# Hybrid decoder layer, one core: when and into which buffers seven weight tiles are split, and the order of the third token tile's normalisation

## The chip, the cores and the metric

One core of one Trainium2 chip. The metric is the device time of one execution in microseconds (us), as the median over runs. A core has a TensorE (PE, matrix multiplications), a VectorE (DVE), a ScalarE (ACT), a GpSimd (POOL) and a SyncE (SP); the last two also issue transfers. Each engine works through its own instruction list in order, so an instruction that waits holds up all that stand behind it on that engine.

## The reference, cut to what matters

One decoder layer on 512 tokens of width 1024, all in float32:

```python
h = layer_norm(x, g_in, b_in)
z = h @ w_in          # split into GLA q, k, v, r, a gate, MLA latents, merge gates g0, g1
y_gla = (gla(...)) @ w_o_gla     # gated linear attention, 4 heads
y_mla = (mla(...)) @ w_o_mla     # latent attention, 8 heads
m = sigmoid(g0) * y_gla + sigmoid(g1) * y_mla
x1 = layer_norm(alpha * x + m @ w_out)
out = layer_norm(alpha * x1 + relu(x1 @ w_ff1) ** 2 @ w_ff2)
```

The parts that matter here are the first `layer_norm` with the latents' product behind it, the two gate products g0 and g1, and the output product of GLA, called yg.

## The kernel before, in words

**Split weights.** TensorE takes every operand as a high and a low part. A weight tile of 128x1024 is loaded (`wraw`, or `wq` when it is kept for later sums), ACT copies it rounded into the high tile (`act(..., AF.Copy)`), DVE subtracts to get the low one (`vtt(..., op=ALU.subtract)`), and three products are made: high with high, high with low, low with high. In the trace every ACT and DVE instruction that goes through a helper carries the helper's line, L111, so they are told apart by tile name. In the products the lines are L313, L314, L315 (tokens by rows, `gemm_tm`), L279, L280, L281 (`gemm_fm`) and L1299, L1300, L1301 (`unit`).

**The stream.** All weight tiles stand in one list, `stream`, in the order of use. `pump(i)`, called when tile i is wanted, loads up to two tiles ahead on SP and splits one tile ahead, or two where the entry says `"ahead": 2`. The pair of tiles that a split writes has a home:

```python
HOME = {"w": ("whi", "wlo"), "r": ("wraw", "wraw"), "a": ("xh", "xl")}
TAG_W = {'wraw': 3, 'whi': 2, 'wlo': 2}
```

Home "w" is a ring of two high and two low buffers: a split must wait until TensorE has read the tile before the last. Home "r" takes two of the three buffers of the raw loads. Home "a" is the large pool, 24 buffers of 128x1024 shared with activations, kept weights and others; a buffer taken from it makes a later user of the same slot wait.

**Seven products for eight.** g0, g1 and yg are made by `unit`: each weight is cut into four blocks and seven products (11, 21, t1, 22, t2, t3, t4) replace eight. The t tiles are sums of blocks. Each product has two tiles, g = 0 and 1, of 24 matmuls each. A sum is made either by DVE (`u_sum`, `wq<-wq,wraw`) or by a transfer on POOL's queue that adds while it writes: `u_load` (L1272 loads, L1274 accumulates) for the t1 and t3 of g1 and yg, and `u_acc` (L394 to L398) which turns g1's t2 into its t4 as soon as t2 has been split.

**Order of the stages around the change.** Token tiles 0 and 1 are normalised and transposed; then the latents' product runs with tokens 0 to 255 (`gemm_tm` with i = 0 and 1) while the generator `ln_in1` normalises tiles 2 and 3 (`ln_rows`: statistics, variance, a power on POOL at L483, the bias `nmr`, then two halves) and transposes them (`ln_transpose`, L505). `ln_in1` also orders two splits behind the variances (`stream[tt + 3]["gates"]`). Stage two, about 250 to 297 us, is g1's products; stage three, to 340 us, is yg's, mixed with the MLA query products (qr, qn, kn, mv). ACT and DVE serve all of them: splits, the gates' activations (`gt`, `u`, `e`) and the operand sums (`hx`, `so`, `ogT`, `hraw`).

Of the kernel before, what the change touches and what calls it, by code (L numbers as in the profile page):

```python
# [19 lines left out]
P = 128  # L20
T = 512
D = 1024
NT = T // P
# [29 lines left out]
def tile_hybrid_block(ctx: ExitStack, tc: tile.TileContext, I, out, dbg=None):  # L53
    nc = tc.nc
# [49 lines left out]
    chain = {}  # L104
# [18 lines left out]
    mm = nc.tensor.matmul  # L123
# [17 lines left out]
    xt = []  # L141
# [12 lines left out]
    ident = ca[:, 0:P]  # L154
    identJ = rev(ident)
# [13 lines left out]
    stream = []  # L169
    st = {"dma": 0, "spl": 0, "gates": ()}  # L170
# [120 lines left out]
        tick(width)  # L291
        return accs

    def gemm_tm(pls, xs, n, evac, width=None, tts=range(NT), guard=None, ks=None, accs=None, new=None, fine=False):
        accs = {} if accs is None else accs
        ticks = [0]
        share = n <= 256 and len(pls) == 1 and len(tts) == NT
        nk = pls[0]["nk"]
        for k in ks or range(nk):
            ws = [weights(pl, k) for pl in pls]  # L300
            first, last = k == 0, k == nk - 1
            for tt in tts:
                c = slice(tt * P, (tt + 1) * P)
                xh, xl = xs[k][:, 0, c], xs[k][:, 1, c]
                for j, (hi, lo) in enumerate(ws):
                    if first:
                        if share and tt % 2:
                            accs[tt, j] = accs[tt - 1, j][:, 256:]
                        else:
                            accs[tt, j] = (new or MM)()  # L310
                    o = accs[tt, j][:, :n]
                    opens = first and not (share and tt % 2)
                    mm(o, xh, hi[:, :n], start=opens, stop=False, skip_group_check=share)  # L313
                    mm(o, xh, lo[:, :n], start=False, stop=False, skip_group_check=share)  # L314
                    mm(o, xl, hi[:, :n], start=False, stop=last, skip_group_check=share)  # L315
                ticks[0] += 1
                if fine is True or fine and ticks[0] % fine == 0:
                    tick(width)
            if not last and not fine:
                tick(width)  # L320
        if evac is None:
            return accs
        if guard:
            guard()
        todo = [(tt, j) for tt in tts for j in range(len(pls))]
        for i, (tt, j) in enumerate(todo):
            evac(tt, j, accs[tt, j])
            if i == len(todo) // 2 - 1:
                pump(pls[-1]["idx"][-1] + 1)
        tick(width)  # L330

    HOMES = "wwrawarawawawa"
    half = LAT // 2
    PL = {}
# [61 lines left out]
    def plan_unit(*seq):  # L396
        for key, op in seq:
            for g in range(UNITS[key][2]):  # L398
                PL[key, op, g] = len(stream)
                e = {"nk": 4, "n": 256, "res": False}  # L400
                if op[0] != "t" and (op, key) not in HELD:
                    e["dmas"] = [(slice(0, 4), u_src(key, int(op[0]) - 1, int(op[1]) - 1, g), None)]
                else:
                    e["src"] = lambda q=(key, (op, g)): WQ[q]
                    if key == "g0" and op in ("t1", "t2"):
                        e["ahead"], e["home"] = 2, "wr"[g]
                if op == ("t1" if key == "g0" else "22"):
                    e["post"] = lambda raw, q=(key, "t1", "t2", g): u_sum(*q, WQ[q[0], ("22", q[3])] if q[0] == "g0" else raw)
                    if key == "f1":
                        e["post2"] = lambda raw, q=(key, "12", "t3", g): u_sum(*q, raw)  # L410
                elif op == "21" and key == "yg":
                    e["post"] = lambda raw, g=g: u_sum("yg", "t2", "t4", g, raw)
                elif op == "t2" and key == "g1":
                    e["post"] = lambda raw, g=g: u_acc("g1", "t2", "t4", g, "21")
                elif op == "t2" and key != "yg":
                    e["post2" if key == "f1" else "post"] = lambda raw, q=(key, "t2", "t4", g): u_sum(*q, WQ[q[0], ("21", q[3])])
                stream.append(e)
# [53 lines left out]
        fb += nb  # L471


    def ln_rows(src, dst, mv, on_act=False, behind=None):
        bst = S([P, 2, 6], F32, "bst")
        for j in range(2):
            with ExitStack() as gates:
                if behind is not None:
                    gates.enter_context(tc.issue_after((behind if j else st["var"]).ins))
                bns(bst[:, j, :], src[:, j * T:(j + 1) * T])  # L480
        bna(mv, bst)
        st["var"] = vts(mv[:, 1:2], mv[:, 1:2], LN_EPS, None, op0=ALU.add)
        st["pow"] = gtt(mv[:, 1:2], mv[:, 1:2], mhalf[:, 0:1], op=ALU.pow)  # L483
        if on_act is not False:
            nmr = S([P, 1], F32, "nmr")
            chain.pop("dve", None)
            behind = st["nmr"] = stt(nmr, mv[:, 0:1], -1.0, mv[:, 1:2], op0=ALU.mult, op1=ALU.mult)
            for j in range(2):
                c = slice(j * T, (j + 1) * T)
                if j in on_act:  # L490
                    st["norm"] = act(dst[:, c], src[:, c], AF.Identity, scale=mv[:, 1:2], bias=nmr)
                else:
                    st["norm1"] = vts(dst[:, c], src[:, c], mv[:, 0:1], mv[:, 1:2], op0=ALU.subtract, op1=ALU.mult)
        else:
            vts(dst, src, mv[:, 0:1], mv[:, 1:2], op0=ALU.subtract, op1=ALU.mult)
        return behind

    def ln_transpose(rows, g, b, outs, hf, alt=False, n="h0"):
        tk = slice(hf * 256, (hf + 1) * 256)
        for k in range(NK):  # L500
            if len(outs) <= k:
                outs.append(A([P, 2, T], F32R, n) if n == "h0" else (B([P, T], F32R, n), B([P, T], F32R, n)))
            p = MM() if alt and k in (4, 5) else PX()
            for i in range(2):
                nc.tensor.transpose(p[:, i * P:(i + 1) * P], rows[2 * hf + i][:, k * P:(k + 1) * P],  # L505
                                    identJ if hf and n == "h0" else ident)
            tmp = B([P, 256], F32, "lnt")
            hi, lo = part(outs[k], 0, tk), part(outs[k], 1, tk)
            ha = act(hi, p[:, :256], AF.Identity, scale=g[:, k:k + 1], bias=b[:, k:k + 1])
            if (alt or n == "h1") and k % 2:  # L510
                act(tmp, p[:, :256], AF.Identity, scale=g[:, k:k + 1], bias=b[:, k:k + 1])
            else:
                vts(tmp, p[:, :256], g[:, k:k + 1], b[:, k:k + 1], op0=ALU.mult, op1=ALU.add)
            hd = vtt(lo, tmp, f(hi), op=ALU.subtract)
            if n == "h1":
                st["ln"] = (ha, hd)
            elif hf and k == 5:
                st["h0"] = (ha, hd)
            yield hd

    mvin = consts.tile([P, NT, 2], F32, name="mvin")
# [106 lines left out]
    def ev_lat(i):  # L628
        def e(a, j, ps):
            if lat[a] is None:  # L630
                lat[a] = A([P, LAT], F32, "lat")
            if a >= 2 and (a + i) % 2 == 0:
                nc.vector.tensor_copy(lat[a][:, i * half:(i + 1) * half], ps[:, :half])
            else:
                act(lat[a][:, i * half:(i + 1) * half], ps[:, :half], AF.Copy)
        return e
# [521 lines left out]
    def ln_in1():  # L1158
        for i in range(4):
            yield  # L1160
        for tt in (2, 3):
            chain.update(dve=st["lo"] if tt == 2 else st["nmr"])
            ln_rows(xt[tt], xt[tt], mvin[:, tt, :], on_act=((0, 1), (0,))[tt - 2])
            chain.clear()
            stream[tt + 3]["gates"] = (st["var"],)
            yield
            if tt == 2:
                yield
        stream[PL["q"]["idx"][0]]["gates"] = (st["norm"],)
        yield from ln_transpose(xt, g_in, b_in, hT, 1, alt=False)  # L1170
# [33 lines left out]
    for hf in range(2):  # L1204
        if hf == 1:
            finish(t_ln1)
            t_prep = spawn(prep())
            t_rp = spawn(r_prep())

        def lat_guard():  # L1210
            finish(t_ln1)
            st["gates"] = st["h0"]
        for i in range(2):
            gemm_tm([PL["lat", i]], hT, half, ev_lat(i), tts=(2 * hf, 2 * hf + 1), guard=lat_guard if i and not hf else None)
    t_lat = spawn(latents())
    t_he = spawn(h_early())
    gemm_fm(PL["q"], hT, T, ev_q)
# [607 lines left out]
```

## Time and profile before

| | us |
|---|---|
| three runs | 867.47, 867.66, 868.06 |
| median | 867.66 |
| the profiled execution | 867.63 |
| its span | 865.8 |
| TensorE busy | 853.8 |
| VectorE busy | 656.5 |
| ScalarE busy | 491.9 |
| GpSimd busy | 136.5 |

Times within the span count from its start. An engine's "idle before" in a row is time after its previous instruction ended; for TensorE, whose matmuls overlap and whose ends are modelled, the distance from one start to the next says more. A 128x256 matmul follows the previous one every 0.12 us, a 128x360 one every 0.165 us and a 128x512 one every 0.23 us where nothing waits.

### The profile page before, as it was taken

Reading aid. Unit: us, or ns where it says so; the run is one execution under the profiler, and the core shown is the slowest. Engines: PE = TensorE matmul, PEld = TensorE weight load, DVE = VectorE, ACT = ScalarE, POOL = GpSimd, SP = SyncE. Lnnn points to the kernel's source line nnn. Section 1 sums busy time; section 2 is a strip of 40 time slices with the busy share of each in tenths; the row PEclk is TensorE's granted clock in tenths of the full one; section 3 lists DMA queues with packets and bytes.
Section 4 is the critical chain, followed back from the end, with each engine's and each line's share of the span. In section 5 each row is a group of like instructions: output and inputs, shape, how many; then the busy total and the mean of one; then the engine's idle time right before and its main releaser. Section 6 shows DMA issues by size and latency. Waiting matters only on the chain.

```text
span 865.8 us, 13210 instructions
## 1 busy us (share of the span) xinstructions
PE 853.8 (99%) x4887; PEld 752.8 (87%) x4887; DVE 656.5 (76%) x1141; ACT 491.9 (57%) x863; POOL 136.5 (16%) x179
## 2 busy tenths in 40 slices
PE   8999999999999999999999999999999999999996
PEld 7988888889999998988888889988888888889985
DVE  7857889977578858897856878985567546888865
ACT  6556977655566754565745334475466446766820
POOL 1530001110221103030000021005301520141000
PEclk9999999999999999999999999999999999999999
DMA  9896946696649916233155355009922990499312
GB/s 317 226 199 175 345 148 167 212 264 209 148 148 238 205 43 171 56 104 98 32 176 217 120 167 190 1 1 267 256 61 51 304 214 16 104 243 232 106 69 75
DMA packets 101231, 137.94 MB, mean 159 GB/s; under 512 B 13201, under 2 KB 66116, under 8 KB 101168
## 3 DMA queue, kind: packets, MB, share of 16 engines
q1 hardware_dynamic: 76512, 91.35, 33.6%
q0 software_dynamic: 22784, 41.10, 22.7%
q10 hardware_dynamic: 1872, 4.66, 1.4%
q8 instruction: 38, 0.62, 0.3%
q14 instruction: 25, 0.20, 0.1%
HBM read 113.49 MB, written 8.91 MB: 141 GB/s over the span
## 4 chain that ended last, share of the span: by engine, by line
PE 95%; DVE 3%; ACT 1%; DMA 0%; issue 0%; POOL 0%; POOLq 0%; DVEq 0%
PE mm L279 10%; PE mm L280 10%; PE mm L281 10%; PE mm L1301 6%; PE mm L1299 6%; PE mm L1300 6%; PE mm L314 5%; PE mm L315 5%; PE mm L313 5%; PE px L1633 3%; PE px L1634 3%; PE px L1635 3%; PE mm L1633 2%; PE mm L1634 2%; PE mm L1635 2%; PE mm L863 1%
## 5 line engine op out<-in xcount | busy, mean ns | idle before, releaser
L111 DVE TENSOR_TENSOR wlo<-wraw,whi 128x1024 fp32r<-128x1024 f32 (+2 forms) x96 | 96.0, 1006 | 65.2 <-ACT whi L111 65.1
L111 ACT ACTIVATE whi<-wraw 128x1024 fp32r<-128x1024 f32 (+2 forms) x96 | 84.1, 884 | 77.2 <-PE mm L280 20.7
L111 DVE TENSOR_TENSOR wlo<-wq,whi 128x1024 fp32r<-128x1024 f32 x52 | 63.6, 1223 | 31.9 <-ACT whi L111 31.7
L280 PE MATMUL mm<-h,whi 128*128 128x512 f32 x224 | 87.2, 389 | 0.0
L279 PE MATMUL mm<-h,whi 128*128 128x512 f32 x224 | 87.1, 390 | 0.0
L281 PE MATMUL mm<-h,wlo 128*128 128x512 f32 x224 | 83.2, 390 | 0.0
L111 ACT ACTIVATE whi<-wq 128x1024 fp32r<-128x1024 f32 x52 | 55.0, 1058 | 33.6 <-PE mm L1300 16.1
L1652 POOL DMA_DIRECT2D res<-ev x42 | 38.4, 1064 | 180.7 <-ACT ev L111 150.0
L1301 PE MATMUL mm<-sh,wlo 128*128 128x256 f32 x176 | 50.0, 284 | 0.3 <-DVE wlo L111 0.2
L1299 PE MATMUL mm<-sh,whi 128*128 128x256 f32 x176 | 50.0, 284 | 0.0
L1300 PE MATMUL mm<-sh,whi 128*128 128x256 f32 x176 | 49.8, 283 | 0.0
L279 PEld LDWEIGHTS mm<-h,whi 128*128 128x128 f32 x224 | 42.1, 188 | 8.8
L281 PEld LDWEIGHTS mm<-h,wlo 128*128 128x128 f32 x224 | 42.0, 188 | 8.7
L280 PEld LDWEIGHTS mm<-h,whi 128*128 128x128 f32 x224 | 42.1, 188 | 8.6
L111 ACT ACTIVATE relu<-mm 128x512 f32<-128x512 f32 x26 | 15.2, 594 | 41.9 <-PE mm L281 41.9
L111 ACT ACTIVATE xh<-wraw 128x1024 fp32r<-128x1024 f32 (+1 forms) x24 | 24.1, 1014 | 26.1 <-PE mm L315 15.2
L111 DVE TENSOR_TENSOR xl<-wraw,xh 128x1024 fp32r<-128x1024 f32 (+1 forms) x24 | 27.9, 1171 | 11.8 <-ACT xh L111 11.8
L1301 PEld LDWEIGHTS mm<-sh,wlo 128*128 128x128 f32 x176 | 33.8, 192 | 0.7 <-DVE wlo L111 0.7
L1300 PEld LDWEIGHTS mm<-sh,whi 128*128 128x128 f32 x176 | 33.8, 192 | 0.0
L1299 PEld LDWEIGHTS mm<-sh,whi 128*128 128x128 f32 x176 | 33.8, 192 | 0.0
L1301 PE MATMUL mm<-h,wlo 128*128 128x256 f32 x112 | 32.1, 287 | 0.0
L1299 PE MATMUL mm<-h,whi 128*128 128x256 f32 x112 | 31.8, 284 | 0.0
(487 smaller groups left out, 2784.0 us busy)
## 6 DMA issues: line engine op xcount, KB each, us to landing
wraw<-in_w_ff_dram SPq DMA_DIRECT2D x36, 512.0 KB, 5.0
wraw<-in_w_in_dram SPq DMA_DIRECT2D x30, 512.0 KB, 5.1
wq<-in_w_ff_dram POOLq DMA_DIRECT2D x26, 512.0 KB, 9.4
res<-ev POOLq DMA_DIRECT2D x42, 256.0 KB, 9.9
wq<-in_w_in_dram POOLq DMA_DIRECT2D x20, 512.0 KB, 10.1
wq<-in_w_in_dram SPq DMA_DIRECT2D x18, 512.0 KB, 7.5
hsd<-hs SPq DMA_DIRECT2D x16, 256.0 KB, 3.9
xr<-hsd SPq DMA_DIRECT2D x16, 256.0 KB, 4.3
```

Source lines behind the costliest of these rows:

```text
L111: ins = op(*a, **k)
L279: mm(o, hi[:, c], xh, start=first, stop=False)
L280: mm(o, hi[:, c], xl, start=False, stop=False)
L281: mm(o, lo[:, c], xh, start=False, stop=last)
L313: mm(o, xh, hi[:, :n], start=opens, stop=False, skip_group_check=share)
L314: mm(o, xh, lo[:, :n], start=False, stop=False, skip_group_check=share)
L315: mm(o, xl, hi[:, :n], start=False, stop=last, skip_group_check=share)
L1299: mm(oa, hi[:, k, c], xh, start=opens and k == 0 and a == 0, stop=False, skip_group_check=True)
L1300: mm(oa, hi[:, k, c], xl, start=False, stop=False, skip_group_check=True)
L1301: mm(oa, lo[:, k, c], xh, start=False, stop=k == 3, skip_group_check=True)
L1633: mm(o, xh[:, c], hi[:, pp], start=opens, stop=False, skip_group_check=True)
L1634: mm(o, xh[:, c], lo[:, pp], start=False, stop=False, skip_group_check=True)
```

## The change: what it does

Three parts.

*Part 1, the third token tile.* In `ln_rows` a call can be put between the power and the bias. For token tile 2, `ln_in1` puts `pump(4)` there, so that stream tiles 5 and 6, latents' weights, are split directly behind that tile's variance and the bias follows the second of them. The tile 6 split was gated on tile 3's variance before. The latents' product with i = 1 gets `held=True`: its last-k matmuls of the first token tile are put behind a certain transpose (`st["tp"]`, the one of k = 1).

*Part 2, six tiles of g1.* All tiles with g = 1 of g1 but t2's (11, 21, t1, 22, t3, t4) are split two ahead instead of one, into the large pool ("xh", "xl") instead of the ring of two.

*Part 3, one tile of yg.* The g = 1 tile of yg's t3 is split into two raw buffers (home "r").

```diff
--- before.py
+++ after.py
@@ gemm_tm
+                held=False):
...
-                    mm(o, xh, hi[:, :n], start=opens, stop=False, skip_group_check=share)
+                    with ExitStack() as gates:
+                        if last and held and tt == tts[0]:
+                            gates.enter_context(tc.issue_after(st["tp"].ins))
+                        mm(o, xh, hi[:, :n], start=opens, stop=False, skip_group_check=share)
@@ plan_unit
+                if key == "g1" and g and op not in ("t2",):
+                    e["ahead"], e["home"] = 2, "a"
+                if (key, op, g) == ("yg", "t3", 1):
+                    e["home"] = "r"
@@ ln_rows(..., between=None)
             chain.pop("dve", None)
+            if between is not None:
+                between()
             behind = st["nmr"] = stt(nmr, mv[:, 0:1], -1.0, mv[:, 1:2], op0=ALU.mult, op1=ALU.mult)
@@ ln_transpose
+            if n == "h0" and k == 1:
+                st["tp"] = tp
@@ ln_in1
+        def splits():
+            stream[5]["gates"] = (st["var"],)
+            pump(4)
+            chain.update(dve=st["lo"])
+
         for tt in (2, 3):
             chain.update(dve=st["lo"] if tt == 2 else st["nmr"])
-            ln_rows(xt[tt], xt[tt], mvin[:, tt, :], on_act=((0, 1), (0,))[tt - 2])
+            ln_rows(xt[tt], xt[tt], mvin[:, tt, :], on_act=((0, 1), (0,))[tt - 2], between=splits if tt == 2 else None)
             chain.clear()
-            stream[tt + 3]["gates"] = (st["var"],)
+            if tt == 3:
+                stream[7]["gates"] = (st["var"],)
@@ the latents' product
-            gemm_tm([PL["lat", i]], hT, half, ev_lat(i), tts=(2 * hf, 2 * hf + 1), guard=lat_guard if i and not hf else None)
+            gemm_tm([PL["lat", i]], hT, half, ev_lat(i), tts=(2 * hf, 2 * hf + 1), guard=lat_guard if i and not hf else None,
+                    held=i and not hf)
```

What this does to the instruction lists shows best at three places. The first is VectorE's list at token tiles 2 and 3 (x_112 and x_114); xl are low parts of the latents' weights, nmr the biases. With + stands what is new, with - what was there.

```order
 L111 TENSOR_SCALAR mvin<-mvin 128x1
-L111 TENSOR_TENSOR xl_300<-wlo_233,xh_299 128x2x360
+L111 TENSOR_TENSOR xl_291<-wlo_233,xh_290 128x2x360
+L111 TENSOR_TENSOR xl_295<-wlo_235,xh_294 128x2x360
 L111 SCALAR_TENSOR_TENSOR nmr_289<-mvin 128x1
-L111 BN_STATS bst_309<-x_114 128x6 x2
-L111 BN_AGGR mvin<-bst_309 128x2
+L111 BN_STATS bst_313<-x_114 128x6 x2
+L111 BN_AGGR mvin<-bst_313 128x2
 L111 TENSOR_SCALAR mvin<-mvin 128x1
-L111 TENSOR_TENSOR xl_328<-wlo_235,xh_327 128x2x360
-L111 SCALAR_TENSOR_TENSOR nmr_315<-mvin 128x1
+L111 TENSOR_TENSOR xl_369<-wraw_237,xh_368 128x2x360
```

The split of wlo_235 (xl_328, now xl_295) moves from behind tile 3's variance to behind tile 2's, ahead of both biases, and that of wraw_237 (xl_369) moves up ahead of tile 3's bias. On TensorE the first four transposes of x_112 move from behind the first two products with wlo_235's tile to behind the first two with wraw_237's; and between the four transposes of x_114 and the next product's first matmul now stand three matmuls (mm_340 with xh_368 and xl_369), where ten stood.

The second place is ScalarE's list at the end of g1. Before, whi_3340 and whi_3385 are the two tiles of g1's t4, made from wq_2529 and wq_2532 after their accumulating transfers, and whi_3421 is the first tile of yg.

```order
L111 ACTIVATE whi_3340<-wq_2529 128x1024
L111 ACTIVATE gt_2724<-u_627_3290,hbg 128x256
L111 ACTIVATE gt_2726<-u_627_3290,hbg 128x256
L111 ACTIVATE ogT_2564<-hx_3334 128x256
L111 ACTIVATE gt_2680<-e_604_3106,hbg 128x2x128
L111 ACTIVATE gt_2682<-e_604_3106,hbg 128x2x128
L111 ACTIVATE whi_3385<-wq_2532 128x1024
L111 ACTIVATE so_3370<-hx_3333 128x512
L111 ACTIVATE gt_2724<-e_611_3146,hbg 128x2x128
L111 ACTIVATE gt_2726<-e_611_3146,hbg 128x2x128
L111 ACTIVATE so_639_3371<-hx_3334 128x256
L111 ACTIVATE whi_3421<-wraw_3383 128x1024
```

In the changed kernel the same piece of ScalarE's list reads so (xh_3344 is the second t4 tile, in the large pool):

```order
L111 ACTIVATE whi_3340<-wq_2529 128x1024
L111 ACTIVATE xh_3344<-wq_2532 128x1024
L111 ACTIVATE u_629_3294<-mm_2902 128x512
L111 ACTIVATE gt_2680<-u_624_3253,hbg 128x256
L111 ACTIVATE gt_2682<-u_624_3253,hbg 128x256
L111 ACTIVATE whi_3421<-wraw_3387 128x1024
L111 ACTIVATE gt_2724<-u_629_3294,hbg 128x256
L111 ACTIVATE gt_2726<-u_629_3294,hbg 128x256
```

The split of t4's second tile stands directly behind the first one's, and yg's first tile whi_3421 only four instructions behind it. On TensorE the first two matmuls that read whi_3421 stand ahead of all of t4, right behind g1's t3, and the rest of that tile between the two t4 tiles. Since the large pool has fewer buffers free, SP issues the loads of yg's t1 and t3 sums later, and on POOL the two accumulating transfers of L394 (g1's t4) now stand ahead of all four of yg.

The third place is ScalarE's list at yg's t3. Before, whi_3768 and whi_3786 are its two tiles, whi_3758 a tile of qr, the query product that runs ahead of it; in the changed kernel the g = 1 tile is wraw_3786.

```order
 L111 ACTIVATE u_684_3696<-mm_3459 128x512
+L111 ACTIVATE wraw_3786<-wq_3384 128x1024
 L111 ACTIVATE whi_3758<-wraw_3701 128x2x256
 L111 ACTIVATE u_688_3734<-mm_3500 128x512
```

```order
-L111 ACTIVATE whi_3768<-wq_3377 128x1024
-L111 ACTIVATE whi_3786<-wq_3380 128x1024
+L111 ACTIVATE whi_3768<-wq_3381 128x1024
+L111 ACTIVATE whi_3860<-wraw_3784 128x256
 L111 ACTIVATE tab_3739<-px_3748 128x512
-L111 ACTIVATE whi_3860<-wraw_3784 128x256
 L111 ACTIVATE q_705_3795<-rt_703_3790 128x512
```

The g = 1 tile is split ahead of qr's second tile and no longer takes a place in the ring; TensorE puts two of its matmuls into qr and the rest ahead of the g = 0 tile, and the next query tiles (whi_3860, whi_3898) move up one place in the ring.

More of the change, by code (lines that the diff above doesn't have):

```diff
@@ L292, in gemm_fm, with gemm_tm @@
         return accs
-    def gemm_tm(pls, xs, n, evac, width=None, tts=range(NT), guard=None, ks=None, accs=None, new=None, fine=False):
+    def gemm_tm(pls, xs, n, evac, width=None, tts=range(NT), guard=None, ks=None, accs=None, new=None, fine=False,
+                held=False):
         accs = {} if accs is None else accs
@@ L471, in tile_hybrid_block, with ln_rows @@
         fb += nb
-    def ln_rows(src, dst, mv, on_act=False, behind=None):
+    def ln_rows(src, dst, mv, on_act=False, behind=None, between=None):
         bst = S([P, 2, 6], F32, "bst")
@@ L504, in ln_transpose @@
             for i in range(2):
-                nc.tensor.transpose(p[:, i * P:(i + 1) * P], rows[2 * hf + i][:, k * P:(k + 1) * P],
-                                    identJ if hf and n == "h0" else ident)
+                tp = nc.tensor.transpose(p[:, i * P:(i + 1) * P], rows[2 * hf + i][:, k * P:(k + 1) * P],
+                                         identJ if hf and n == "h0" else ident)
+            if n == "h0" and k == 1:
+                st["tp"] = tp
             tmp = B([P, 256], F32, "lnt")
```

## The prediction, made before the result was seen

> **What bounds the kernel now.** I read the page's chain that ended last first, then TensorE's list of waits, then the timeline around each wait. The chain, by engine:
>
> ```profile
> PE 95%; DVE 3%; ACT 1%; DMA 0%; issue 0%; POOL 0%; POOLq 0%; DVEq 0%
> ```
>
> So the time is TensorE's, and it falls only where TensorE stops standing. Of its waits, outermost engine and line first, then the total in us, three of the smallest lie in the stages that the change touches:
>
> ```profile
> PE mm L314 <- DVE wlo L111: 0.2, 1, 0.2
> PE mm L1299 <- ACT whi L111: 0.2, 1, 0.2
> PE mm L1301 <- DVE wlo L111: 0.2, 1, 0.2
> ```
>
> This view understates: it counts from the modelled end of one matmul to the next start. In the timeline I take start to start instead. TensorE's rows in the latents' product, and then at two g = 1 tiles of g1:
>
> ```profile
> 23.80 0.60 PE L505 MATMUL px<-ca,x 128*128 128x128 f32 x4
> 24.78 0.43 PE L314 MATMUL mm<-xl,h 128*128 128x360 f32 x1 [0.38 <-DVE xl L111]
> 25.05 0.33 PE L315 MATMUL mm<-xh,h 128*128 128x360 f32 x1
> 25.22 0.33 PE L314 MATMUL mm<-xl,h 128*128 128x360 f32 x1
> ```
>
> ```profile
> 275.90 0.28 PE L1300 MATMUL mm<-sh,whi 128*128 128x256 f32 x1
> 276.33 0.39 PE L1301 MATMUL mm<-sh,wlo 128*128 128x256 f32 x1 [0.15 <-DVE wlo L111]
> 276.55 0.28 PE L1299 MATMUL mm<-sh,whi 128*128 128x256 f32 x1
> ```
>
> ```profile
> 279.19 0.28 PE L1300 MATMUL mm<-sh,whi 128*128 128x256 f32 x1
> 279.60 0.39 PE L1301 MATMUL mm<-sh,wlo 128*128 128x256 f32 x1
> ```
>
> From 275.90 to 276.33 are 0.43 us where 0.12 is the pace of this shape without a wait (296.73 to 296.85, further down), so 0.31 is lost; the next start comes 0.22 later instead of 0.12, another 0.10. A wait that the list calls 0.15 costs 0.41. At 279.60 it is 0.29 + 0.10 = 0.39. The view has one entry for this line, so that second stall does not stand in it at all. At 24.78 the view's idle time is 0.38; by starts, four transposes some 0.11 apart from 23.80 should have been followed at 24.24: 0.54 lost, and 0.10 behind it (0.27 to the next start, then 0.17, the pace of 128x360).
>
> I make the sum against the profiled execution, 867.63 us with a span of 865.8, so 1.8 lies outside the span and stays. It lies 0.03 below the median of 867.66. The waits further on hang on work that itself follows TensorE's, so they move along, and what is won goes to the end undiminished.
>
> **Part 1, the third token tile.** VectorE and ScalarE there:
>
> ```profile
> 23.74 0.15 DVE L111 TENSOR_SCALAR mvin<-mvin 128x1 f32<-128x1 f32 x1
> 23.82 0.91 DVE L111 TENSOR_TENSOR xl<-wlo,xh 128x720 fp32r<-128x720 f32 x1
> 25.17 0.22 DVE L111 SCALAR_TENSOR_TENSOR nmr<-mvin 128x1 f32<-128x1 f32 x1 [0.44 <-POOL mvin L483]
> ```
>
> ```profile
> 26.15 1.04 ACT L111 ACTIVATE whi<-wraw 128x1024 fp32r<-128x1024 f32 x1
> 27.18 1.93 ACT L111 ACTIVATE h<-px,ca 128x256 fp32r<-128x256 f32 x4
> ```
>
> The split at 23.82, for which TensorE waits at 24.78, moves a whole token tile up (its inputs are loaded and its high part was made early), so 0.54 + 0.10 = 0.64 goes. In exchange tile 2's bias comes behind two splits, about 0.28 later, since the power on POOL hid most of the split; tile 3's statistics, its variance (24.02) and its bias (25.45, by the same 1.43 from variance to bias) follow. ScalarE's wide weight split goes from 26.15 to 26.43, an evacuation of the latents' product (about 0.45) now stands ahead of h, and h starts about 27.93 instead of 27.18, ready at 28.5. TensorE used to have ten matmuls (10 x 0.165 = 1.65; 24.78 to 25.22 shows 0.17) between its last transposes and the first reader of h; now three (0.5). Without a wait it would reach that reader at 28.2; it waits till 28.55, and with the 0.10 behind a wait 0.4 is given back. **Net 0.25.** The cover is those three matmuls: if h is later by x, x is lost whole. Bounds: all of the 0.64, if h is in time, and -0.2, if ScalarE runs half a microsecond later.
>
> **Part 2, the g = 1 tiles of g1.** Split two ahead into the large pool they no longer wait in the ring or directly behind the g = 0 tile and its sum. The stalls at 276.33 and 279.60 go: 0.41 + 0.39 = **0.80**. A third is the first tile of yg, whose low part comes late behind DVE's other work:
>
> ```profile
> 296.73 0.28 PE L1299 MATMUL mm<-ogT,whi 128*128 128x256 f32 x1
> 296.85 0.28 PE L1300 MATMUL mm<-ogT,whi 128*128 128x256 f32 x1
> 297.13 0.39 PE L1301 MATMUL mm<-ogT,wlo 128*128 128x256 f32 x1
> ```
>
> 0.28 less 0.12 is 0.16, and 0.10 behind it: **0.26**. In the new order the low part is not needed until a whole t4 tile (24 matmuls, 2.9 us) after the high one. What is late next: I walked the other tiles of g1 through the new order and found none late, the tightest t3's g = 0 low part, which has DVE's sums ahead of it; so I cost the rest at nothing, and up to 0.3 if that cover is gone.
>
> But the part also adds a wait. t4's second tile is split by ScalarE directly behind the first; its source is an accumulating transfer on POOL's queue. Behind that split are queued u, two gates and the split of yg's first tile, and TensorE's order puts two matmuls with that tile ahead of all of t4. Durations of those ScalarE instructions, with the place in the trace where TensorE goes from t3 to t4, and the accumulates:
>
> ```profile
> 285.30 1.06 ACT L111 ACTIVATE whi<-wq 128x1024 fp32r<-128x1024 f32 x1 [0.98 <-PE mm L1300]
> 286.26 0.58 ACT L111 ACTIVATE u<-mm 128x512 f32<-128x512 f32 x1
> 286.74 0.90 ACT L111 ACTIVATE gt<-u,hbg 128x256 f32<-128x256 f32 x2
> ```
>
> ```profile
> 290.98 0.28 PE L1299 MATMUL mm<-h,whi 128*128 128x256 f32 x1
> ```
>
> ```profile
> L394 POOL DMA_DIRECT2D wq<-in_w_in_dram x2: 1283/1283/1283, 279.8 to 282.0; - x2
> ...
> DMA to landing us min/median/max: 6.1/7.0/7.9
> ```
>
> By the pitches of these rows (0.96 for the split, 0.48 for u, 0.4 for a gate) the split of yg's first tile ends 0.96 + 0.48 + 0.8 + 1.06 = 3.3 us after the accumulate has landed. The accumulate can be issued when t2's second tile has been split, which is about 279.9: some 2 us before the second of the trace's two, at 282.0, because one tile fewer goes through the ring ahead of it. TensorE, with 0.8 saved before, wants yg's tile at 290.98 - 0.8 = 290.18 (part 1 shifts both sides alike). So there is no stall if the accumulate takes at most 290.18 - 3.3 - 279.9 = 7.0 us. Of the two in the trace one took 6.1, the other, sharing with the first and with loads, 7.9. The new one shares with the two loads of yg's t1 that the fuller pool moves to 279 to 282; I take 7.9: a stall of 7.9 - 7.0 = 0.9. Bounds: nothing, and, by accumulates that ran wholly beside loads,
>
> ```profile
> wq<-in_w_in_dram POOLq DMA_DIRECT2D x2, 512.0 KB, 11.9
> ```
>
> (issues from 254 to 262), 11.9 - 7.0 = 4.9. The likely value is nearer to the low end since only two loads run beside. **-0.9.**
>
> The Trainium skill, "DMA: Bandwidth & Descriptors", section "Anatomy of one DMA — SWDGE (gpsimd) path", fits a GpSimd-issued DMA as 2.0 us plus its bytes at 436 GB/s, which for 512 KB makes an estimate of 3.2 us. By that the accumulate would be early by far and the sum 0.9 larger; the trace's 6.1 to 11.9 disagree with it.
>
> **Part 3, yg's t3, g = 1.** The rows of qr and t3, then of qn and of the first value product:
>
> ```profile
> 321.13 0.40 PE L280 MATMUL mm<-latT,whi 128*128 128x512 f32 x1
> 321.52 0.50 PE L281 MATMUL mm<-latT,wlo 128*128 128x512 f32 x1
> 321.86 0.40 PE L279 MATMUL mm<-latT,whi 128*128 128x512 f32 x1
> ```
>
> ```profile
> 325.63 0.28 PE L1300 MATMUL mm<-ogT,whi 128*128 128x256 f32 x1
> 326.15 0.39 PE L1299 MATMUL mm<-ogT,whi 128*128 128x256 f32 x1 [0.24 <-ACT whi L111]
> ```
>
> ```profile
> 332.00 0.40 PE L280 MATMUL mm<-latT,whi 128*128 128x512 f32 x1
> 332.23 0.39 PE L281 MATMUL mm<-latT,wlo 128*128 128x512 f32 x1
> 332.58 0.50 PE L279 MATMUL mm<-latT,whi 128*128 128x512 f32 x1
> 332.91 0.39 PE L280 MATMUL mm<-latT,whi 128*128 128x512 f32 x1
> ```
>
> ```profile
> 338.83 0.40 PE L313 MATMUL mm<-whi,latT 128*128 128x256 f32 x2
> 339.47 0.39 PE L314 MATMUL mm<-wlo,latT 128*128 128x256 f32 x1 [0.25 <-DVE wlo L111]
> ```
>
> With a 128x512 pace of 0.23 (332.00 to 332.23), 321.13 to 321.86 is 0.73 for 0.46: 0.27 lost for qr's low part. Two t3 matmuls now stand in that gap. At 326.15 it is 0.52 for 0.12, 0.40 and 0.10 behind: the ring of two had just been freed. The g = 1 tile no longer uses the ring and was split before, so 0.50 goes. From 332.23 to 332.91 it is 0.68 for 0.46, 0.22 for a ring place that is now one tile earlier. At 339.47 it is 0.64 for 0.24, 0.40 and 0.10: its low part stood on DVE behind e and gt. One place earlier in the ring it is ready over 1 us sooner: 0.50. Sum 0.27 + 0.50 + 0.22 + 0.50 = **1.5**. What hides the new work: the tile's source, whose load now starts about 290.2 when t3 of g1 has been read, plus an accumulate of even 11.9 behind a load of as much lands by 314, ahead of about 317 when ScalarE takes it. The two raw buffers that it takes hold back the next query tiles' loads until t3 has been read; these are small and are wanted some 4 us later. Bounds: -0.3, if such a load comes late and the waits only change places, and 1.5.
>
> **The sum.** 0.25 + 0.80 + 0.26 - 0.9 + 1.5 = 1.9. From 867.63 to 865.7 us (0.22%). About 0.2% (1.7 us) is what a measurement of this kernel tells from no change, so the border to "faster" is at 865.9.
>
> **Rivals.** *B, the accumulate is in time* (6.1 us, as the quicker row): no new stall, 0.9 more, 864.8. For it: only one accumulate precedes it on its queue, and that three microseconds earlier; against it: two loads move beside it. The Trainium skill's figure above leads to the same outcome. Chance 0.2.
>
> *C, slower: ScalarE stands behind the accumulate.* If the transfer takes 11.9 us, as between 254 and 262, ScalarE's list is blocked to 291.8 and yg's first tile comes at 295.1, a stall of 4.9 and the sum 2.8 - 4.9 = -2.1: 869.7. It turns slower than before from 2.8 + 7.0 = 9.8 us on. For it: the same kind of transfer did take that long, and what stands behind the wait is now wanted early. Against it: only two loads run beside it. The same page of the Trainium skill, section "SWDGE vs HWDGE vs iDMA", says each DMA engine takes turns between its queues, so that accumulate and loads would share evenly; that would lengthen the accumulate only while the loads last, which no row of this trace shows by itself. Chance 0.13.
>
> *D, part 3 does little.* The query tiles still wait, for the ring or DVE's order, so the waits move along instead of going: 0.25 + 0.80 + 0.26 - 0.9 = 0.4, 867.2. For it: they are four waits with three different causes; against it: in the new order every one of these splits stands earlier. Chance 0.14.
>
> **How the numbers follow.** The forecast (A) has the rest, 0.53; its own range is 864.9 to 866.5 with part 1 between 0 and 0.5 and a stall between 0.3 and 1.4. The range takes in B, with part 1 at its upper end (864.4), and D, with part 1 at its lower end and the accumulate a little longer (868.0). Only C, and a little of D, is left out. Faster by over 0.2% is all of B and some six tenths of A: 0.5. Slower by over 0.2% (above 869.4) is most of C: 0.11. The rest, 0.39, is within.
>
> **What would show it.** In the changed trace: no gap before the first L314 on the tile 6 low part, and a short one after the second transposes; pace 0.12 at the g = 1 tiles of g1; one gap of about 0.9 at the step from t3 to t4 with ScalarE's split of yg's first tile as the releaser and idle time of ScalarE for a DMA ahead of it; pace at qr, at t3, qn and the value product. I am wrong if the gap at t4 is above 2 us or missing, or if two or more gaps stay between 318 and 341 us.

## The result: slower by 4 us, and where it stands in the profile

The changed kernel takes 871.71 us (median of 6 runs, 871.22 to 872.42) against 867.70 for the kernel before (6 runs, 867.23 to 868.06): ratio 1.0047, 95% interval 1.0034 to 1.0060. The forecast was 865.7, with a range of 864.4 to 868.0. The profiled execution took 871.95 us with a span of 870.2, 4.4 more than before. Further below, one run of the kernel with u first and two of the kernel before took 8 to 39% longer at a lower granted clock; the ratios leave them out.

TensorE's list of waits has one new entry, at its head, and no longer any of the three that the prediction quoted:

```profile
PE mm L1319 <- ACT u L111: 4.5, 1, 4.5
```

(L1319 to L1321 are now the lines of `unit`'s three matmuls, L317 to L319 those of `gemm_tm`.) So a gap at the end of g1 was foreseen, but not this one: TensorE waits for u, not for the split of yg's first tile. TensorE's rows there:

```profile
287.14 0.28 PE L1321 MATMUL mm<-sh,wlo 128*128 128x256 f32 x1
291.91 0.58 PE L1319 MATMUL mm<-sh,xh 128*128 128x256 f32 x1 [4.49 <-ACT u L111]
292.30 0.42 PE L1320 MATMUL mm<-sh,xh 128*128 128x256 f32 x1
292.51 0.41 PE L1321 MATMUL mm<-sh,xl 128*128 128x256 f32 x1
292.72 0.41 PE L1319 MATMUL mm<-sh,xh 128*128 128x256 f32 x1
```

At 287.14 starts the last matmul of t3's g = 0 tile and at 291.91 the first of its g = 1 tile: 4.77 us instead of 0.12, so 4.65 lost. Two places further the rows show a second loss: these matmuls follow each other every 0.21 us where 0.12 was the pace. The chain that ended last, from the start of the transfer on, names who held whom (start, length, what):

```profile
280.08 9.88 DMA wq<-in_w_in_dram
...
290.32 0.13 ACT xh L111
290.45 0.83 issue
291.28 0.59 ACT u L111
291.87 0.04 issue
291.91 0.58 PE mm L1319
```

The accumulate of t4's second tile takes 9.88 us. ScalarE stands for it with the split (xh), and only then comes u. u is the copy out of the bank that holds the sum up to t2's g = 1 products. t3's g = 1 tile adds its own products to the sum in that same bank, so TensorE may not start until u has read it. The windows view of the stretches before, in and behind the slow matmuls (after the time: busy time of PE, PEld, DVE, ACT, POOL, then the granted clock, the share and GB/s of the transfers):

```profile
283.00:287.20 4.20, 4.20 (x37) 4.20 (x36) 4.20 (x7) 2.07 (x4) 0.79 (x1) 1.00 1.01 188
291.90:297.20 5.30, 5.29 (x24) 5.29 (x25) 4.22 (x6) 3.60 (x8) 0.65 (x1) 0.50 0.69 106
297.20:302.00 4.80, 4.80 (x41) 4.80 (x41) 2.12 (x5) 1.52 (x3) 0.00 (x0) 1.00 0.74 229
```

For the 24 matmuls behind the gap the granted clock was 0.50. They took 5.29 us instead of 24 x 0.12 = 2.88: 2.41 more. The Trainium skill, "TensorE: Matmul & The Clock Gate", section "What's actually happening", says that TensorE's clock falls to half after a window of about 3.4 us without work and comes back after one of sustained work; this trace agrees (0.50 for 5.3 us behind a gap of 4.5, then 1.00). Behind its start the kernel before has no gap above 1.3 us that could show it.

The parts of the forecast that were gains are there. In the windows of g1's stalls and of yg's t3, first of the kernel before and then of the changed one, TensorE's busy time in the first column no longer falls short of the stretch:

```profile
275.00:284.00 9.00, 8.71 (x70) 8.30 (x70) 7.74 (x13) 4.60 (x7) 2.57 (x2) 1.00 1.00 218
320.00:341.00 21.00, 20.52 (x120) 17.13 (x119) 16.04 (x27) 12.58 (x21) 4.51 (x9) 1.00 0.55 155
```

```profile
275.00:284.00 9.00, 9.00 (x77) 9.00 (x76) 8.59 (x15) 3.84 (x6) 2.58 (x2) 1.00 0.79 162
325.50:347.00 21.50, 21.50 (x137) 19.09 (x137) 18.10 (x30) 11.97 (x21) 6.47 (x13) 1.00 0.64 175
```

In the latents' product the gap at the transposes of x_112 is gone, and the one behind those of x_114 has come, as forecast:

```profile
25.95 0.60 PE L515 MATMUL px<-ca,x 128*128 128x128 f32 x4
26.31 0.41 PE L318 MATMUL mm<-xl,h 128*128 128x360 f32 x1
...
27.54 0.60 PE L515 MATMUL px<-ca,x 128*128 128x128 f32 x4
27.89 0.41 PE L317 MATMUL mm<-xh,h 128*128 128x360 f32 x1
28.14 0.33 PE L318 MATMUL mm<-xl,h 128*128 128x360 f32 x1
28.31 0.33 PE L319 MATMUL mm<-xh,h 128*128 128x360 f32 x1
28.72 0.43 PE L317 MATMUL mm<-xh,h 128*128 128x360 f32 x1
28.99 0.33 PE L318 MATMUL mm<-xl,h 128*128 128x360 f32 x1
```

At 26.31 a product follows the four transposes at once. Behind those at 27.54 come three matmuls, then 0.41 to the reader of h instead of 0.165, and 0.10 behind it: 0.35 given back, 0.4 forecast.

The account of the span: 4.65 + 2.41 lost, about 1.06 (part 2's three stalls), 1.5 (part 3) and some 0.1 (part 1) won: +4.4, which is the difference measured in the profiled executions. The first two are read from the rows above; how the 2.7 won is shared among the parts is tested below.

### The profile page after: what moved, and what is told of

Same layout as the page of the kernel before. It is cut to its first block, busy times and chain, and to the rows that moved or that the text cites. A ratio compares the mean times of both kernels' runs of the same rounds, so it can differ in the third digit from the quotient of the medians.

```text
span 870.2 us, 13203 instructions
## 1 busy us (share of the span) xinstructions
PE 855.7 (98%) x4887; PEld 755.5 (87%) x4887; DVE 655.9 (75%) x1141; ACT 491.9 (57%) x863; POOL 136.0 (16%) x179
## 4 chain that ended last, share of the span: by engine, by line
PE 95%; DMA 2%; DVE 2%; ACT 1%; issue 0%; POOLq 0%; POOL 0%; DVEq 0%; ACTq 0%
PE mm L279 10%; PE mm L280 10%; PE mm L281 10%; PE mm L319 5%; PE mm L317 5%; PE mm L318 5%; PE mm L1319 5%; PE mm L1321 5%; PE mm L1320 5%; PE px L1654 3%; PE px L1655 3%; PE px L1653 2%; PE mm L1654 2%; PE mm L1655 2%; PE mm L1653 2%; PE mm L875 1%
## 5 line engine op out<-in xcount | busy, mean ns | idle before, releaser
L111 DVE TENSOR_TENSOR wlo<-wraw,whi 128x1024 fp32r<-128x1024 f32 (+1 forms) x93 | 92.3, 999 | 65.6 <-ACT whi L111 65.5
L111 ACT ACTIVATE whi<-wraw 128x1024 fp32r<-128x1024 f32 (+1 forms) x93 | 80.9, 878 | 78.1 <-issue 20.6
L111 DVE TENSOR_TENSOR wlo<-wq,whi 128x1024 fp32r<-128x1024 f32 x48 | 58.7, 1223 | 28.2 <-ACT whi L111 28.0
L111 ACT ACTIVATE whi<-wq 128x1024 fp32r<-128x1024 f32 x48 | 50.7, 1057 | 27.6 <-PE mm L1320 17.4
L1319 PE MATMUL mm<-sh,whi 128*128 128x256 f32 x152 | 43.2, 284 | 0.0
L1320 PE MATMUL mm<-sh,whi 128*128 128x256 f32 x152 | 43.0, 283 | 0.0
L1321 PE MATMUL mm<-sh,wlo 128*128 128x256 f32 x152 | 43.0, 283 | 0.0
L1320 PEld LDWEIGHTS mm<-sh,whi 128*128 128x128 f32 x152 | 29.2, 192 | 0.0
L1321 PEld LDWEIGHTS mm<-sh,wlo 128*128 128x128 f32 x152 | 29.2, 192 | 0.0
L1319 PEld LDWEIGHTS mm<-sh,whi 128*128 128x128 f32 x152 | 29.2, 192 | 0.0
L1321 PE MATMUL mm<-h,wlo 128*128 128x256 f32 x96 | 27.6, 287 | 0.0
L1319 PE MATMUL mm<-h,whi 128*128 128x256 f32 x96 | 27.3, 284 | 0.0
```

The source lines that it names most:

```text
L111: ins = op(*a, **k)
L1319: mm(oa, hi[:, k, c], xh, start=opens and k == 0 and a == 0, stop=False, skip_group_check=True)
L1320: mm(oa, hi[:, k, c], xl, start=False, stop=False, skip_group_check=True)
L1321: mm(oa, lo[:, k, c], xh, start=False, stop=k == 3, skip_group_check=True)
```

## The experiments

The theory: ScalarE's list is the cause. The split that waits for the accumulate stands ahead of u, and u holds TensorE's bank; the gap is long enough to halve the clock. The rivals: that the large pool and the loads which it pushes back cost the time; that the forecast wait (yg's first tile) is the true bound and u only stands in front of it; that the half clock has another reason than the gap. All kernels of a group ran on one chip with the kernel before; the ratios are to it.

| kernel | median us | before | ratio, 95% interval |
|---|---|---|---|
| t4's g = 1 tile in the ring | 866.18 | 867.81 | 0.9982 (0.9974 to 0.9991) |
| u ahead of that split | 869.03 | 867.81 | 1.0007 (0.9998 to 1.0017) |
| 19 added matmuls | 870.96 | 867.81 | 1.0039 (1.0023 to 1.0054) |
| yg's loads later | 869.06 | 867.81 | 1.0011 (1.0001 to 1.0021) |
| part 1 alone | 867.54 | 867.72 | 0.9999 (0.9990 to 1.0008) |
| part 2 alone | 873.95 | 867.72 | 1.0071 (1.0058 to 1.0085) |
| part 3 alone | 866.09 | 867.72 | 0.9981 (0.9972 to 0.9990) |
| ring, split behind u's gates | 866.34 | 867.72 | 0.9986 (0.9978 to 0.9995) |
| pool, split behind u's gates | 865.14 | 867.69 | 0.9970 (0.9959 to 0.9981) |
| changed kernel again | 870.98 | 867.69 | 1.0041 (1.0028 to 1.0055) |
| 19 added matmuls again | 870.01 | 867.69 | 1.0030 (1.0020 to 1.0040) |
| 12 added matmuls | 869.96 | 867.69 | 1.0031 (1.0018 to 1.0044) |

### One tile back in the ring

```diff
-                if key == "g1" and g and op not in ("t2",):
+                if key == "g1" and g and op not in ("t2", "t4"):
```

> The changed kernel, but g1's t4, g = 1, stays in the ring of two and is split one ahead; the other five tiles stay two ahead in the large pool. Theory (ScalarE's evacuation u of the bank that g1's t3, g = 1, writes is queued behind t4's split, which waits for the accumulate): u comes ahead of that split again, so the 4.6 us of standing and the half-clock stretch behind it (24 matmuls at 0.213 instead of 0.120, 2.4 in all) go: 871.7 - 7.0 = 864.7 us. Rival (the large pool and the loads that it pushes back are what costs): five of six tiles stay there, so some 871 us.

866.18 us, so 5.5 of the 7.0 came back with this one tile (the changed kernel's 871.71 was taken apart from this group, but the kernel before differs by only 0.1 between the two), though five of six tiles stayed in the pool and yg's loads went out as early as in the changed kernel (279.3 and 281.6). The rival is out. u is done before the split, and the gap at t3 is gone. Of the 1.5 that lack to 864.7, 1.1 is a new gap at yg's g = 1 tile:

```profile
296.22 0.28 PE L1320 MATMUL mm<-ogT,whi 128*128 128x256 f32 x1
297.37 0.39 PE L1319 MATMUL mm<-ogT,whi 128*128 128x256 f32 x1 [0.87 <-ACT whi L111]
```

1.15 instead of 0.12, and 0.10 behind it. TensorE's order has two matmuls of yg's g = 1 tile right behind the first two of its g = 0 tile, and that tile's split is late.

### u first, the rest as changed

```diff
-                    act(u2[g], o, AF.Copy)
+                    ui = act(u2[g], o, AF.Copy)
+                    if key == "g1" and g:
+                        stream[PL["g1", "t4", 1]]["gates"] = (ui,)
```

> The changed kernel with one order added: t4's g = 1 split comes behind the evacuation u on ScalarE, still ahead of the gates and of yg's first tile, and still waits for the accumulate. Theory: t3's g = 1 tile starts on time (no gap at 287), but now the wait that was forecast shows: yg's first tile is split some 3.2 us after the accumulate's landing at 290, about 293.1, where TensorE wants it at 290.1: a gap of 3.0, with or without a half-clock stretch behind it: 867.6 to 870.0 us. Rival (u was the only wait): 864.7 us.

869.03 us, within the theory's 867.6 to 870.0. TensorE's rows, then the accumulates' times to landing and the clock behind the gap:

```profile
290.12 0.28 PE L1321 MATMUL mm<-sh,xl 128*128 128x256 f32 x1
294.15 0.43 PE L1319 MATMUL mm<-ogT,whi 128*128 128x256 f32 x1 [3.75 <-ACT whi L111]
```

```profile
DMA to landing us min/median/max: 6.1/8.6/11.0
```

```profile
294.10:297.90 3.80, 3.75 (x18) 3.75 (x19) 2.83 (x5) 1.91 (x5) 1.58 (x2) 0.55 1.18 260
```

With u out of the way, TensorE does t3's g = 1 tile on time and then stands at exactly the place that the prediction had named, for yg's first tile: 4.03 instead of 0.12, and half clock behind it. (The profiled execution took 870.47 us, 1.4 above the median; the last section comes back to this.) The accumulate took 11.0 us here; the prediction's rule, time less 7.0, gives 4.0, and 3.9 was lost. So the forecast wait was real. It did not show in the changed kernel because another reader of the same list came first. "u was the only wait" is out.

### Work for TensorE in the gap

```diff
+                        with ExitStack() as gates:
+                            if (key, op, g, k, a) == ("g1", "t3", 1, 0, 0):
+                                fill = PX(n="fill")
+                                w = stream[PL["g1", "t3", 0]]["w"][0]
+                                for n in range(19):
+                                    with tc.issue_after((fi if n else lm).ins):
+                                        fi = mm(fill, w[:, 0, 0:P], w[:, 0:2, :].rearrange("p k n -> p (k n)"), start=True, stop=True)
+                                gates.enter_context(tc.issue_after(fi.ins))
+                            mm(oa, hi[:, k, c], xh, start=opens and k == 0 and a == 0, stop=False, skip_group_check=True)
...
-                        mm(oa, lo[:, k, c], xh, start=False, stop=k == 3, skip_group_check=True)
+                        lm = mm(oa, lo[:, k, c], xh, start=False, stop=k == 3, skip_group_check=True)
```

> The changed kernel with 19 matmuls of 128x512 added that TensorE makes between t3's two tiles, into a bank that nobody reads, so that it is busy for 4.4 of the 4.6 us in which it stands. Theory (the half clock comes from the standing): u comes no earlier, but t3's g = 1 tile then runs at 0.12 a matmul and the granted clock stays 1.00: 871.7 - 2.4 = 869.3 us. Rival (the slow pace has to do with that tile, its place in the large pool or the transfers beside it): it stays at 0.21, 871.7 us or more.

```profile
286.95 4.50 PE L1325 MATMUL fill<-whi 128*128 128x512 f32 x19
291.50 0.38 PE L1327 MATMUL mm<-sh,xh 128*128 128x256 f32 x1
291.72 0.28 PE L1328 MATMUL mm<-sh,xh 128*128 128x256 f32 x1
291.83 0.28 PE L1329 MATMUL mm<-sh,xl 128*128 128x256 f32 x1
```

The window of the tile:

```profile
291.50:294.30 2.80, 2.80 (x23) 2.80 (x24) 2.80 (x5) 2.80 (x8) 0.63 (x1) 1.00 0.60 88
```

u came no earlier (the accumulate took 9.8 us), but the tile ran at 0.12 a matmul, at a granted clock of 1.00, with the same tile in the same buffer and the same transfers beside it. So the gap makes the half clock. On the size the medians do not follow: 870.96, only 0.8 below the changed kernel's 871.71, while the span of the profiled execution, the fastest of four, is 868.0, 2.2 below. The two kernels again, on one chip:

> The kernel with 19 added matmuls once more, with more rounds, since four times spread over 2 us: its trace was 2.2 us shorter in span than the changed kernel's while the median was only 0.8 lower. Theory (half clock is worth 2.4): 869.3 us, 2.4 below the changed kernel on this chip. Rival (0.8 is all): 870.9 us.

> The changed kernel once more, unaltered, on the same chip as the others of this group: 871.7 us, for the distance to the two kernels with added matmuls.

870.01 (10 runs, 869.10 to 872.55) and 870.98 (5 runs, 870.46 to 872.10): 1.0 less, not 2.4. In the trace the half-clock stretch is gone in this run too. What the medians lack shows in part behind the stage, in waits that the changed kernel's two traces do not have. The first row is of this run (871.65 us), the second of the first run with 19 (869.79):

```profile
524.99 0.44 PE L515 MATMUL px<-ca,res 128*128 128x128 f32 x2 [0.61 <-ACT lnt L111]
```

```profile
782.69 0.39 PE L1329 MATMUL px<-h,wlo 128*128 128x256 f32 x1 [0.37 <-DVE wlo L111]
```

Lined up matmul by matmul with the trace of the last kernel below, which has no gap here (the added matmuls left out), the changed kernel's two traces lose 7.08 and 6.83 us between 286 and 300 us and the two with 19 added lose 4.63 and 5.07: 2.45 and 1.76 less. This run then loses 1.2 near 524 us and 0.4 near 784, the first run with 19 loses 0.6 near 782. So at its place the half clock costs about 1.8 to 2.5 us, and some of that is lost again far behind. What causes those later waits, and how often they come, no run shows.

With 12 instead of 19:

> As before with 12 matmuls, so that TensorE stands for about 1.9 us of the 4.6. A gap of 0.9 us (first experiment) left the granted clock at 1.00, one of 2.5 (loads later) was followed by 1.6 us at full pace and then 3.2 at half. Theory (it takes a stretch without work of about 2.5 us or more): the clock stays 1.00, time as with 19. Rival (any gap over 1 us will do): a half-clock stretch of 3 us or more behind the gap, some 871 us.

```profile
287.22 2.91 PE L1325 MATMUL fill<-whi 128*128 128x512 f32 x12
291.41 0.39 PE L1327 MATMUL mm<-sh,xh 128*128 128x256 f32 x1 [1.28 <-ACT u L111]
291.63 0.28 PE L1328 MATMUL mm<-sh,xh 128*128 128x256 f32 x1
```

In the profiled execution TensorE stood for 1.28 us, and the pace behind it was 0.12: not every gap over 1 us brings the half clock. That execution is the fastest of five (869.07, mean granted clock 0.999); the slowest took 871.86 at 0.996, and since it has no rows, it stays open whether the half clock was there. The median is 869.96, as with 19.

### The accumulate without yg's loads beside it

```diff
-        if op in ("t2", "t3"):
-            u_load("yg", {"t2": "t1", "t3": "t3"}[op])
+        if op == "t3":
+            u_load("yg", "t1")
+            u_load("yg", "t3")
```

> The changed kernel with the loads of yg's t1 sums called after g1's t3 instead of after t2, so that none of them runs beside g1's accumulate. Theory (the accumulate takes 9.9 us because two loads run beside it): it takes 6 to 6.5 us, lands near 286.4, u is out by 289.3 and the gap at t3's g = 1 tile shrinks from 4.6 to about 2; yg's t1 may come late instead. Rival (it is the queue's own pace behind another accumulate): 9.9 us stays, and the gap.

The accumulates' times to landing, TensorE's row at the gap, and the windows behind it:

```profile
DMA to landing us min/median/max: 5.9/6.6/7.3
```

```profile
290.19 0.38 PE L1319 MATMUL mm<-sh,xh 128*128 128x256 f32 x1 [2.54 <-ACT u L111]
```

```profile
290.20:291.80 1.60, 1.60 (x12) 1.60 (x13) 1.60 (x3) 1.60 (x4) 0.65 (x1) 0.92 0.48 71
291.80:295.00 3.20, 3.20 (x17) 3.20 (x16) 2.65 (x5) 1.98 (x6) 0.00 (x0) 0.51 0.78 177
295.00:300.00 5.00, 5.00 (x44) 5.00 (x43) 4.48 (x9) 3.52 (x7) 1.59 (x2) 1.00 1.15 307
```

The second accumulate took 7.3 us instead of 9.9, the gap fell from 4.5 to 2.5, and the time to 869.06. The gap fell by less than the accumulate because in this order another split stands between it and u on ScalarE:

```profile
288.61 1.04 ACT L111 ACTIVATE whi<-wq 128x1024 fp32r<-128x1024 f32 x1
```

The accumulate did not reach the 6 to 6.5 us expected: one of the loads was issued at 284.2 all the same and ran beside its last part. The edit also moved something else: in the changed kernel yg's first accumulate was issued at 286.41, on the same queue and while t4's was still under way, and here only at 289.56. So the 2.6 of the 9.9 belong to the loads and to that accumulate together, and no run parts the two. The theory, that what runs beside it makes it slow, is right in kind; its size is open. In the kernels with two or more loads and that accumulate beside it, it took 9.4 to 11.0 us. The Trainium skill, "DMA: Bandwidth & Descriptors", section "SWDGE vs HWDGE vs iDMA", has each DMA engine take turns between its queues; that the accumulate gets faster when transfers beside it go away (9.9 to 7.3) agrees with it.

### Each part alone

Part 1 alone (the diff's changes to `gemm_tm`, `ln_rows`, `ln_transpose`, `ln_in1` and the latents' call), part 2 alone (the first two added lines of `plan_unit`), part 3 alone (the other two):

> The kernel before with part 1 alone. Theory, by the changed kernel's trace: the 0.65 at xl goes, but 0.24 comes at the second split's low part and 0.36 behind the last transposes: -0.1 to -0.3, so 867.5 us, no difference that shows. The prediction on record had 0.25 for it. Rival (part 1 has a share in the loss): over 868.5 us.

> The kernel before with part 2 alone. Theory: all of the loss is here, 4.65 of standing and 2.4 of half clock less the 1.06 of three stalls that go: 867.7 + 6.0 = 873.7 us. Rival (parts 1 or 3 bring some of it, by their order or their buffers): below 872 us.

> The kernel before with part 3 alone. Theory (the four stalls between 320 and 340 are real time and go): 867.7 - 1.5 = 866.2 us. Rival (they only move, or work behind them hides them): within 0.3 us of 867.7.

867.54, 873.95 and 866.09 us against 867.72: -0.2, +6.2 and -1.6. The three theories held within 0.3 us, and the rivals fell. The sum is +4.4, where the whole change gave +4.0: the parts do not hinder each other. With part 3 alone TensorE has no gap in its stretch any more:

```profile
320.00:342.00 22.00, 22.00 (x141) 19.58 (x140) 18.88 (x31) 12.14 (x21) 6.96 (x14) 1.00 0.66 174
```

### Taking the split out of the way

First with the tile in the ring, as in the first experiment, and its split behind the gates that read u:

```diff
-        act(g, ps, AF.Tanh, scale=0.5, bias=hbg[:, br * NK + m:br * NK + m + 1])
+        st["gt"] = act(g, ps, AF.Tanh, scale=0.5, bias=hbg[:, br * NK + m:br * NK + m + 1])
...
                     evac(1, 0, g, u2[g], True)
+                    if key == "g1" and g:
+                        stream[PL["g1", "t4", 1]]["gates"] = (st["gt"],)
```

> The kernel of the first experiment (t4's g = 1 tile in the ring) with one order added: its split on ScalarE comes behind the two gates of u, where it came ahead of them and stood 3 us for the accumulate. Theory (what is left of the loss there is ScalarE's list behind the waiting split, 0.9 + 0.1 + 0.1 at yg's g = 1 tile): that tile's split comes 0.9 earlier, and 1.0 less than 866.2 is 865.2 us. Rival (the wait is for the load of that tile or the ring): 866.2 stays.

My theory fell: 866.34, no gain. ScalarE and TensorE at yg's g = 1 tile:

```profile
296.31 1.06 ACT L111 ACTIVATE whi<-wraw 128x1024 fp32r<-128x1024 f32 x1 [0.71 <-ACT so L111]
```

```profile
297.42 0.39 PE L1319 MATMUL mm<-ogT,whi 128*128 128x256 f32 x1 [0.84 <-ACT whi L111]
```

ScalarE was free 0.7 us before and did not start, and the tile's load had been issued by 276. 296.31 is when TensorE has made the last matmuls of t4's g = 1 tile, whose buffers in the ring of two this split needs. So it is the ring that makes this gap, as the rival had it, and the tile belongs into the pool; the next run tests that. The profiled execution, 867.44 us and so 1.1 above the median, has another gap of 0.9 at 307.3, for the low part of a later tile, which the first experiment's has not; its cause stays open. Then, with the tile in the pool as in the changed kernel and the same added order:

> The changed kernel with one order added: the split of t4's g = 1 tile, in the large pool, comes behind the two gates of u on ScalarE, and so behind u and behind yg's first tile. Theory: nothing that TensorE wants early stands behind the accumulate any more, and the ring is free for yg's tiles: no gap from 270 to 320 us; 871.7 - 7.0 = 864.7 us, faster than both kernels. Rival (the pool or the pushed-back loads bring a wait of their own once this one is gone): 866 us or more, with a gap at another tile.

```profile
287.52 1.06 ACT L111 ACTIVATE whi<-wraw 128x1024 fp32r<-128x1024 f32 x1 [0.54 <-ACT gt L111]
288.59 0.91 ACT L111 ACTIVATE gt<-u,hbg 128x256 f32<-128x256 f32 x2
290.10 1.06 ACT L111 ACTIVATE xh<-wq 128x1024 fp32r<-128x1024 f32 x1 [0.60 <-DMA wq<-in_w_in_dram]
```

```profile
270.00:285.00 15.00, 15.00 (x128) 15.00 (x127) 13.55 (x21) 8.11 (x14) 2.58 (x2) 1.00 0.65 146
285.00:300.00 15.00, 15.00 (x128) 15.00 (x127) 14.13 (x24) 11.41 (x22) 5.14 (x4) 1.00 1.09 258
300.00:320.00 20.00, 20.00 (x165) 19.50 (x163) 12.00 (x16) 11.08 (x17) 0.00 (x0) 1.00 0.74 147
```

865.14 us (7 runs, 864.57 to 865.42), 0.4 above the 864.7 expected, and below both kernels: ratio 0.9970 to the kernel before, 5.8 us under the changed kernel on the same chip. The accumulate took 9.9 us here too. It costs nothing, since ScalarE waits for it 0.6 us with nothing behind that TensorE wants early. One order of one instruction was worth 5.8 us.

## Why the prediction was wrong

**The step that failed** is the term -0.9 of the sum, for the stall behind t4's accumulate; 4.65 + 2.41 = 7.06 was measured for it. The working goes wrong in part 2 at this step: "Behind that split are queued u, two gates and the split of yg's first tile, and TensorE's order puts two matmuls with that tile ahead of all of t4." The list was right and u stands in it, but only its last member was priced. For each instruction behind a wait one has to ask when its own reader wants it. u's reader is the first matmul of t3's g = 1 tile, by the changed trace at 287.26, 2.9 us ahead of the 290.18 at which yg's tile was wanted; and it starts 1.95 us after the landing (289.96 to 291.91), where yg's tile needs 3.3. The point from which the accumulate decides was thus 287.26 - 1.95 - 280.08 = 5.2 us, not 7.0. None of t4's accumulates in any trace was that short: the least was 5.9. By this estimate even the row of 6.1, which the prediction held for harmless (rival B), would give a stall of 0.9. That u was the first wait, and that yg's tile is only the second, is shown by the experiment with u first, where the gap moves to yg's tile and has the size of the prediction's rule.

**The size of the accumulate** was 9.9 where 7.9 was taken: the two loads and yg's accumulate beside it cost more than the row of before with less beside it (7.3 to 9.9 by the experiment with the loads later). The 5.2 is made from the same trace as the 4.65, so that they fit is no test; two other traces are one: 10.1 - 5.2 = 4.9 where the changed kernel's second run lost 4.86, and 9.8 - 5.2 = 4.6 where part 2 alone lost 4.56.

**The price of a gap** was taken as its length. Behind 4.65 us of standing the clock was half for 24 matmuls, 2.41 more. The prediction had no term for it; the trace of before has no gap that long behind its start.

Of the 6.0 us between forecast and result, the longer accumulate is some 2.0 by the prediction's own rule (9.9 - 7.0 = 2.9 instead of 0.9), the earlier reader 1.75 (4.65 instead of 2.9) and the clock 2.41; no single one makes the miss.

**Rival C** had the right mechanism (ScalarE's list blocked behind the accumulate) with a chance of 0.13, but the wrong reader. At 9.9 us its rule turns to loss only just (the boundary was 9.8); the measured loss is from u and the clock.

**Right were** part 1 (0.25 forecast, 0.2 by itself, not to be told from nothing), part 2's three stalls (gone in the windows, the third in the last kernel's from 285 to 300 us) and part 3 (1.5 forecast, 1.6 by itself). Rival D is out. Without the one wait the forecast sum would have been 2.8 less than before, and the last kernel, which takes just that wait away, is 2.55 below.

## What to carry to other kernels

When a change puts an instruction that waits for a transfer further up in an in-order list, go through all that stand behind it, and price each by the time at which its own reader wants it: a copy out of an accumulation bank is wanted as soon as the next product is to be added in that bank, which can be earlier than any split. A gap of TensorE may cost more than its length: in these traces it did from 2.54 us on. And a tile that is split early costs nothing if its split is ordered behind what others wait for: the buffer and the place in the list are two decisions.

## What the runs showed of the hardware

In the profiled executions the half clock came after 4.5, 3.75 and 2.54 us of TensorE's standing (by the waits), and not after 0.87 or 1.28. After 2.54 it came late: 1.6 us at full pace first (0.92 granted), then 3.2 us at 0.51. After the two longer gaps it was there at once and lasted 5.3 and 3.8 us. The Trainium skill, "TensorE: Matmul & The Clock Gate", section "HAM oscillation — how this bites in real kernels", puts the limit for a gap at about 3.4 us; here 2.54 was enough.

It need not come in every execution. With u first, five runs with a mean granted clock of 0.996 took 869.00 to 870.47 us and four with 0.998, a value that the kernel before shows too (0.997 to 0.999), took 866.93 to 867.77. That fits a half-clock stretch in about half of them, at a price of some 2 us; only the run of 870.47 has rows to show it.
